# Modulation sums by block transposition, and a new first phase, in a two-block fp32 sequence kernel

## The chip, the core and the metric

One core of one Trainium2 chip runs the whole program. The metric is the device time of the core in microseconds (us), the median of several executions; beside it stands one profiled execution whose trace is read here. TensorE (PE) multiplies, VectorE (DVE) and ScalarE (ACT) work on rows of 128 partitions, GpSimd (POOL) does the few powers, SyncE (SP) issues the DMAs.

## The reference, cut to what matters

512 tokens, 1024 features, fp32, two blocks one after the other. Each block is modulated by six rows of 1024 values, made from one vector c:

```python
mod = (jax.nn.silu(c) @ w_ada[i] + b_ada[i])[:, None, :]          # w_ada: 1024 x 6144
shift_m, scale_m, gate_m, shift_f, scale_f, gate_f = jnp.split(mod, N_MOD, axis=-1)
h = rmsnorm(x, norm_mix_w[i]) * (1.0 + scale_m) + shift_m
x = x + gate_m * hybrid_mixer(h, w_in[i], conv_w[i], ...)          # proj = h @ w_in: 1024 x 8224
h = rmsnorm(x, norm_mlp_w[i]) * (1.0 + scale_f) + shift_f
x = x + gate_f * (jnp.square(jax.nn.relu(h @ w_up[i])) @ w_down[i])
...
# second block: the same form with token_mixer (mLSTM and sliding-window attention) and conv_ffn
```

The mixer of the first block is a chunked state-space scan in four groups, each with its own B, C and four x tiles, all columns of `proj`.

## The kernel before

Everything is one core's stream of matmuls. Activations stand transposed: a tile `H[j]` holds 128 features by 512 tokens. For accuracy each operand is split into a high and a low fp32r part (`hilo`, L240: ScalarE writes `whi`, VectorE `wlo`), and every product is three matmuls (`hh,whi`, `hl,whi`, `hh,wlo`) of 128x128 weights on 512 columns. An output tile of 128 columns over eight k-tiles is 24 of them. `split_w` loads 256 columns of a weight matrix into the buffers "raw" (four of them), splits them into the rings "hi" and "lo" (five each), and calls `pump`. The framework orders the instructions of each engine when the program is built, by priorities and dependences; each engine then runs its list in order.

**Modulation.** A weight matrix of 25 MB times one vector is done on VectorE: `ada_steps` (L146) takes 256 columns of w_ada in two pieces of 512 KB and adds k-tile by k-tile, scaled by silu(c), into `adacc` (128 partitions x 256), one piece at each call of `ada_next`, which `pump` and `gemm_full` make. What remains is the sum over 128 partitions. `ada_sum` (L160) takes two such `adacc`, that is four column tiles: four fp32 matmuls with a block of ones (32 columns of weights, 128 columns of data) on TensorE, a copy by ScalarE, a transposition by TensorE and an addition of the bias by VectorE into `mod`. The six rows of both blocks, without the first block's first two, are 40 units of 256 columns, so 20 such sums; `ada_until(block, row)` completes a row where it is needed.

**First phase.** The first two rows are needed before anything else. `first_ada(j)` loads their columns of k-tile j (four DMAs of 256 KB), `first_mod(j)` (L494) adds them on VectorE into two `adacc` and sums on TensorE, then copies, transposes, adds the bias and forms the gain `gm_col`. x arrives as eight DMAs of 256 KB on SyncE's queue, behind the first four of w_ada; each 128 tokens are squared and summed (ScalarE), raised to -1/2 (GpSimd), scaled to x-hat (VectorE). `h_tile` (L419) transposes x-hat's tile j on TensorE into `nps` and scales and shifts it into `H[j]`. The loop over j (L533) then adds k-tile j to six output tiles at once (B, C and the four x tiles of group 0), 18 matmuls at L544, four accumulators in PSUM buffers "pg", two in "ps" (four buffers each; `nps`, `adaps` and `colps` use "ps" too).

**After it.** Groups 0 to 3 of the scan are woven with matmuls: `xbc_items(g + 1)` makes the next group's B, C and x tiles, and `LATE` says how many of the seven remaining pool items go into each group as filling. Then follow the branch and output matrices, the MLP, and the second block in the same manner. At w_out (`gemm_full`, `script1`) the tiles of 128 tokens are normalised and transposed one by one for the MLP's first matmuls.

Of the kernel before, what the change touches and what calls it, by code (L numbers as in the profile page):

```python
# [14 lines left out]
P = 128  # L15
# [11 lines left out]
def hybrid_kernel(  # L27
# [70 lines left out]

    K = const("consts", [P, C_NEG])
    stA = stage([rows(a) for a in (c, c_2, norm_mix_w, b_ada)])  # L100
# [13 lines left out]
    xa = x.rearrange("o (t p) (q n) -> p (o t) q n", p=P, n=512)  # L114
    first_raw = [first_ada(0)]
    X = []
    for t in range(NCH):
        row = []
        for q in range(2):
            u = U("x")  # L120
            dma(out=u, in_=xa[:, t, q])
            row.append(u)
        X.append(row)
    dma(out=K[:, C_TRI:C_LAST], in_=consts[:, C_TRI:C_LAST])
# [6 lines left out]
    mhalf = const("mhalf", [P, 16])  # L131
    G.memset(mhalf, -0.5)
# [12 lines left out]

    def ada_steps(ci, col):  # L146

        acc = small("adacc", [P, 2 * P], bufs=ADB)
        for k0 in (0, 4):
            raw = RAW([P, 4, 2 * P])  # L150
            dma(out=raw, in_=ada_w[ci][0, k0 * P:(k0 + 4) * P, col * P:(col + 2) * P].rearrange("(k p) n -> p k n", p=P))
            for k in range(4):
                s_ = csil[:, 8 * ci + k0 + k:8 * ci + k0 + k + 1]
                if k0 + k == 0:
                    V.tensor_scalar(out=acc, in0=raw[:, k], scalar1=s_, scalar2=None, op0=ALU.mult)
                else:
                    V.scalar_tensor_tensor(out=acc, in0=raw[:, k], scalar=s_, in1=acc, op0=ALU.mult, op1=ALU.add)  # L157
            yield acc

    def ada_sum(ci, col, accs):  # L160

        ps = PS("adaps")
        for j in range(4):
            PE.matmul(ps[j * 32:(j + 1) * 32, 0:P], lhsT=ones[:, 0:32], rhs=accs[j // 2][:, j % 2 * P:(j % 2 + 1) * P],  # L164
                      start=True, stop=True)
        row = small("colraw", [P, P])
        act(out=row, in_=ps[:, 0:P], func=AF.Copy)
        yield
        ps = PS("adaps")
        PE.transpose(ps[:, 0:P], row, ident)  # L170
        V.tensor_tensor(out=mod[ci][:, col:col + 4], in0=ps[:, 0:P:32], in1=bcol[ci][:, col:col + 4], op=ALU.add)
        yield

    ada_todo = [(0, 8 * sec + i) for sec in (2, 4, 3, 5) for i in range(0, 8, 2)] + [(1, i) for i in range(0, 48, 2)]
    ada_now, ada_open, ada_half = [], [], []
# [8 lines left out]
    def ada_close(n):  # L184
        while ada_half:
            next(ada_half.pop(0))
        while len(ada_open) > max(n, 1):
            (ci, col), a0 = ada_open.pop(0)
            ada_half.append(ada_sum(ci, col, (a0, ada_open.pop(0)[1])))
            next(ada_half[-1])  # L190
        while ada_half and n == 0:
            next(ada_half.pop(0))

    def ada_next(hold=False):
        if ada_now:
            key, gen = ada_now.pop()
            ada_open.append((key, next(gen)))
            return
        if not hold:
            ada_close(3)  # L200
        if ada_todo and len(ada_open) < ADB - 1:
            ci, col = ada_todo.pop(0)
            ada_now.append(((ci, col), ada_steps(ci, col)))
            next(ada_now[0][1])

    def ada_until(ci, sec):
        todo = [(ci, 8 * sec + i) for i in range(0, 8, 2)]
        while any(t in todo for t in ada_todo + [t for t, _ in ada_now]):
            ada_next()
        ada_close(0)  # L210
# [271 lines left out]
    first = [wi[:, 4096:5120].rearrange("k (s g n) -> k s g n", s=2, n=P)[:, :, 0], wi[:, 2048:2560]]  # L482

    def first_w(j):
        raw = RAW([P, 768])
        o = 0
        for w in first:
            n = w.shape[-1] * (2 if len(w.shape) == 3 else 1)
            dst = raw[:, o:o + n]
            dma(out=dst.rearrange("p (s n) -> p s n", s=2) if len(w.shape) == 3 else dst, in_=w[j * P:(j + 1) * P])  # L490
            o += n
        return raw

    def first_mod(j):  # L494
        src = [first_raw[j][k // 4][:, k % 4] for k in range(8)]
        acc = [small("adacc", [P, 2 * P], bufs=ADB) for _ in range(2)]
        for k in range(8):
            c_, t = csil[:, k:k + 1], acc[k % 2]
            if k < 2:
                V.tensor_scalar(out=t, in0=src[k], scalar1=c_, scalar2=None, op0=ALU.mult)  # L500
            else:
                V.scalar_tensor_tensor(out=t, in0=src[k], scalar=c_, in1=t, op0=ALU.mult, op1=ALU.add)
        ps = PS("adaps")
        for k in range(2):
            for i in range(2):
                PE.matmul(ps[i * 64:(i + 1) * 64, 0:P], lhsT=ones[:, 0:64], rhs=acc[k][:, i * P:(i + 1) * P],
                          start=k == 0, stop=k == 1)
# [13 lines left out]
    for t in range(NCH):  # L521
        rs.append(rsqrt(row_ss(X, t), D, 1e-5, "n"))
        if t:
            xh[t - 1] = x_hat(X, t - 1, rs[t - 1], False)
# [8 lines left out]
    for j in range(8):  # L533
        if j < 7:
            raws.append(first_w(j + 1))
# [1179 lines left out]
```

## Time and profile before

| | us |
|---|---|
| median of 3 runs (1624.26 to 1624.70) | 1624.59 |
| the profiled execution's own time | 1624.09 |
| its span, first to last instruction | 1622.3 |
| TensorE matmuls busy, x7810 | 1589.5 |
| VectorE busy, x1995 | 1086.5 |
| ScalarE busy, x1275 | 715.4 |
| GpSimd busy, x47 | 28.3 |

Busy times of engines overlap. Matmuls are pipelined: each row's duration is longer than its distance to the next, so the distance between starts is the price of one in the stream. PEld are the loads of weights, beside the matmuls. The granted clock is full (0.999 in the mean).

### The profile page before, as it was taken

How to read it: one execution, taken by the hardware profiler on the slowest of the kernel's cores; microseconds unless marked ns; L12 is line 12 of the kernel's file. 1: busy time of each engine (PE TensorE's matmuls, PEld its weight loads, DVE VectorE, ACT ScalarE, POOL GpSimd, SP SyncE). 2: the span in 40 equal slices, each digit the busy share in tenths (PEclk: the TensorE clock that was granted, in tenths of full speed). 3: DMA queues.
4: the chain of work that ended last, by engine and by line, in shares of the span. 5: the costliest groups of instructions: out<-in, count | busy, mean ns of one | idle time of the engine just before them, and what ended most of it. 6: DMA issues, size and time to landing. Idle time of an engine off the chain costs nothing.

```text
span 1622.3 us, 20792 instructions
## 1 busy us (share of the span) xinstructions
PE 1589.5 (98%) x7810; PEld 1274.0 (79%) x7810; DVE 1086.5 (67%) x1995; ACT 715.4 (44%) x1275; POOL 28.3 (2%) x47
## 2 busy tenths in 40 slices
PE   5999999999999999999999999999999999999998
PEld 3778777777877878877877788887788888888886
DVE  6686897888766675876257773578876756145644
ACT  4543656555454332633214332655555643144421
POOL 0000000000000000000000000000011000000000
PEclk9999999999999999999999999999999999999999
DMA  9731544444444435466236571122331323332321
GB/s 280 197 100 59 178 142 149 130 143 138 149 130 138 142 127 177 137 196 209 96 115 197 195 252 48 53 81 76 94 102 53 103 81 102 91 104 87 96 91 53
DMA packets 206830, 206.45 MB, mean 127 GB/s; under 512 B 11469, under 2 KB 184585, under 8 KB 206729
## 3 DMA queue, kind: packets, MB, share of 16 engines
q1 hardware_dynamic: 206729, 205.12, 41.6%
q8 instruction: 61, 1.00, 0.3%
q14 instruction: 40, 0.33, 0.1%
HBM read 202.90 MB, written 2.19 MB: 126 GB/s over the span
## 4 chain that ended last, share of the span: by engine, by line
PE 90%; DVE 4%; DMA 3%; ACT 2%; issue 1%; SPq 0%; POOL 0%; DVEq 0%; POOLq 0%; ACTq 0%
PE ga L274 53%; PE gb L352 21%; PE gb L312 5%; PE go L1494 2%; PE ga L544 2%; DMA wraw<-in_w_ada_dram 1%; DMA AB<-acs 1%; DVE wlo L244 1%; PE nps L424 1%; PE yps L829 1%; PE stps L838 0%; ACT arel L803 0%; PE yps L834 0%; DMA x<-in_x_dram 0%; PE adaps L164 0%
## 5 line engine op out<-in xcount | busy, mean ns | idle before, releaser
L274 PE MATMUL ga<-hh,whi 128*128 128x512 f32 (+1 forms) x1200 | 464.6, 390 | 1.0 <-ACT hh L431 0.9
L244 DVE TENSOR_TENSOR wlo<-wraw,whi 128x1024 fp32r<-128x1024 f32 (+3 forms) x249 | 297.9, 1198 | 246.8 <-ACT whi L243 246.2
L274 PE MATMUL ga<-hl,whi 128*128 128x512 f32 (+1 forms) x1200 | 457.6, 382 | 2.2 <-DVE hl L433 2.1
L274 PE MATMUL ga<-hh,wlo 128*128 128x512 f32 (+1 forms) x1200 | 456.8, 382 | 0.0
L243 ACT ACTIVATE whi<-wraw 128x1024 fp32r<-128x1024 f32 (+3 forms) x249 | 257.5, 1036 | 335.3 <-PE gb L352 151.4
L274 PEld LDWEIGHTS ga<-hh,whi 128*128 128x128 f32 x1200 | 224.1, 188 | 54.1 <-issue 6.7
L274 PEld LDWEIGHTS ga<-hl,whi 128*128 128x128 f32 x1200 | 225.3, 188 | 50.6 <-issue 3.3
L274 PEld LDWEIGHTS ga<-hh,wlo 128*128 128x128 f32 x1200 | 225.3, 188 | 46.7
L157 DVE SCALAR_TENSOR_TENSOR adacc<-wraw,csil,adacc 128x256 f32<-128x256 f32 x280 | 133.7, 482 | 36.1 <-DMA wraw<-in_w_ada_dram 31.7
L352 PE MATMUL gb<-whi,hidh 128*128 128x512 f32 x240 | 78.2, 396 | 0.0
L352 PE MATMUL gb<-wlo,hidh 128*128 128x512 f32 x240 | 77.8, 394 | 0.0
L352 PE MATMUL gb<-whi,hidl 128*128 128x512 f32 x240 | 77.5, 394 | 0.0
L450 DVE SCALAR_TENSOR_TENSOR xs<-xraw,colB,xs 128x511 f32<-128x511 f32 (+2 forms) x72 | 53.8, 748 | 8.8 <-ACT xs L448 7.9
L352 PE MATMUL gb<-whi,fh 128*128 128x512 f32 x176 | 57.3, 396 | 0.0
L352 PE MATMUL gb<-wlo,fh 128*128 128x512 f32 x176 | 57.2, 395 | 0.0
L352 PE MATMUL gb<-whi,fl 128*128 128x512 f32 x176 | 57.0, 394 | 0.0
L352 PEld LDWEIGHTS gb<-whi,hidh 128*128 128x128 f32 x240 | 45.0, 188 | 10.8 <-issue 0.4
L803 ACT ACTIVATE arel<-AB,acs 128x128 f32<-128x128 f32 x128 | 40.7, 389 | 29.0 <-DMA AB<-acs 20.6
L352 PEld LDWEIGHTS gb<-whi,hidl 128*128 128x128 f32 x240 | 45.1, 188 | 10.7
L352 PEld LDWEIGHTS gb<-wlo,hidh 128*128 128x128 f32 x240 | 45.1, 188 | 10.4
L274 PE MATMUL ga<-yh,whi 128*128 128x512 f32 x128 | 51.1, 399 | 0.0
L274 PE MATMUL ga<-yh,wlo 128*128 128x512 f32 x128 | 50.6, 395 | 0.0
(421 smaller groups left out, 2374.2 us busy)
## 6 DMA issues: line engine op xcount, KB each, us to landing
wraw<-in_w_ada_dram SPq DMA_DIRECT2D x80, 512.0 KB
wraw<-in_w_in_dram SPq DMA_DIRECT2D x72, 512.0 KB
wraw<-in_w_down_dram SPq DMA_DIRECT2D x54, 512.0 KB
wraw<-in_w_up_dram SPq DMA_DIRECT2D x88, 256.0 KB
wraw<-in_w_up_dram SPq DMA_DIRECT2D x32, 512.0 KB
araw<-in_w_ada_dram SPq DMA_DIRECT2D x32, 256.0 KB
AB<-acs SPq DMA_DIRECT2D x32, 256.0 KB
wraw<-in_w_branch_ssd_dram SPq DMA_DIRECT2D x16, 512.0 KB
```

What stands on the lines that cost most here:

```text
L157: V.scalar_tensor_tensor(out=acc, in0=raw[:, k], scalar=s_, in1=acc, op0=ALU.mult, op1=ALU.add)
L243: act(out=hi, in_=raw, func=AF.Copy)
L244: V.tensor_tensor(out=lo, in0=raw, in1=f(hi), op=ALU.subtract)
L274: PE.matmul(ps[:, n0:n1], lhsT=a[:, m * P:(m + 1) * P], rhs=b[:, n0:n1], start=i == 0, stop=i == 3 * n - 1)
L312: PE.matmul(pss[t][:, 0:ncols], lhsT=a[:, t * P:(t + 1) * P], rhs=b, start=k == 0 and j == 0, stop=k == n - 1 and j == 2)
L352: PE.matmul(pss[t][q], lhsT=a, rhs=w[b][q], start=i == 0 and j == 0, stop=i == n - 1 and j == 2)
L424: PE.transpose(ps[:, i * P:(i + 1) * P], xh[t][j // 4][:, (j % 4) * P:(j % 4 + 1) * P], ident)
L450: V.scalar_tensor_tensor(out=o[:, d:], in0=ps[:, 0:S - d], scalar=cols[taps - 1 - d], in1=o[:, d:], op0=ALU.mult, op1=ALU.add)
L544: PE.matmul(fps[i], lhsT=a[:, i * P:(i + 1) * P], rhs=b, start=j == 0 and q == 0, stop=j == 7 and q == 2)
L803: act(out=t[:, i * P:(i + 1) * P], in_=AB[q][:, i * P:(i + 1) * P], func=AF.Relu, scale=-1.0, bias=acs[:, hh:hh + 1])
L829: PE.matmul(ps[r * 64:(r + 1) * 64, j * P:(j + 1) * P], lhsT=xdt[:, hh * 64:(hh + 1) * 64], rhs=M[hh // 4][:, (hh % 4) * P:(hh % 4 + 1) * ...
L1494: PE.matmul(opss[t][q], lhsT=x_, rhs=w[q][b_], start=half == 0 and k == 0 and j == 0, stop=half == 1 and k == 3 and j == 2)
```

## The change

The sum over partitions behind the start: a unit is now 512 columns (four pieces); VectorE transposes the 128x512 `adacc` in blocks of 32x32 and adds within each block (`adR`, 16 values a partition), so that each of four groups of 32 partitions holds a partial sum. `ada_until` adds the four with one fp32 matmul of 32 columns for a whole row of 1024 (weights `quarters`), and three small VectorE steps pick each partition's own column and add the bias.

The first phase: x of tokens 0 to 255 comes by ScalarE's queue ahead of everything, the rest on SyncE's behind the first w_ada; ScalarE's table is loaded early by a small Tanh. Statistics are made for two groups of 128 tokens at a time, half of the squares on VectorE. The modulation of k-tiles 0 and 1 is done by TensorE straight from w_ada (`first_pe`: 16 matmuls with 128x128 of w_ada as weights on one column of silu(c)); that of the later ones by ScalarE (one step) and VectorE (seven) into one `adacc`, two k-tiles ahead, with two matmuls on one column for the sum (`first_sum`) that need no transposition. The matmuls of k-tile 0 run first for tokens 0 to 255, then for 256 to 511. There are seven output tiles instead of six (B of group 1 is the seventh), three of them in "ps"; `xbc_items(1)` makes one tile less, and `LATE` gives group 0 four pool items instead of three, group 1 three instead of four.

```diff
+    load_x((0, 1), SC.dma_start)
...
     def ada_steps(ci, col):
+        acc = U("adacc")
+        for h in range(2):
+            a = acc[:, h * 2 * P:(h + 1) * 2 * P]
+            for k0 in (0, 4):
+                raw = RAW([P, 4, 2 * P])
...
+                if h and k0:
+                    tr = U("adtr")
+                    V.transpose(out=tr, in_=acc)
+                    V.tensor_reduce(out=adR[ci][:, col * 4:col * 4 + 16], in_=tr.rearrange("p (b f) -> p b f", f=32),
+                                    axis=AX.X, op=ALU.add)
+                yield
...
     def ada_until(ci, sec):
...
-        ada_close(0)
+        ps = PS("adaps")
+        PE.matmul(ps[:, 0:32], lhsT=quarters, rhs=adR[ci][:, sec * 32:sec * 32 + 32], start=True, stop=True)
...
+    NF = 7
...
+    def first_acc(j):
+
         src = [first_raw[j][k // 4][:, k % 4] for k in range(8)]
+        acc = small("adacc", [P, 2 * P], bufs=ADB)
+        act(out=acc, in_=src[0], func=AF.Copy, scale=csil[:, 0:1])
+        for k in range(1, 8):
+            V.scalar_tensor_tensor(out=acc, in0=src[k], scalar=csil[:, k:k + 1], in1=acc, op0=ALU.mult, op1=ALU.add)
+            if k == 4:
+                yield acc
+        yield acc
+
+    def first_sum(j, acc):
+
+        ps = PS("adaps")
+        for i in range(2):
+            PE.matmul(ps[:, i:i + 1], lhsT=acc[:, i * P:(i + 1) * P], rhs=ones[:, 0:1], start=True, stop=True)
+        first_mod(j, ps)
+
+    def first_pe(j):
+
+        ps = PS("adaps")
         for k in range(8):
...
+                PE.matmul(ps[:, i:i + 1], lhsT=first_raw[j][k // 4][:, k % 4, i * P:(i + 1) * P], rhs=csil[:, k:k + 1],
+                          start=k == 0 and i == 0, stop=k == 7 and i == 1)
+        first_mod(j, ps)
...
+    fps = [PG("ga") for _ in range(4)] + [PS("ga") for _ in range(NF - 4)]
...
     first_raw.append(first_ada(1))
...
+    rs[0] = first_stats((0, 1))
+    first_pe(0)
+    first_hat((0, 1), 0, (1,))
+    first_h(0, (0, 1), False)
+    ws = hilo(raws[0], [P, NF * P])
+    rs[1] = first_stats((2, 3))
+    first_hat((2, 3), 0, (3,))
+    first_mm(0, ws, range(NF), 0, 256)
+    first_h(0, (2, 3), False)
+    raws.append(first_w(1))
     first_raw.append(first_ada(2))
+    first_mm(0, ws, range(NF), 256, S)
+    first_pe(1)
     for j in range(8):
+        if j < 6:
+            raws.append(first_w(j + 2))
+            if j < 5:
+                first_raw.append(first_ada(j + 3))
+            acc = first_acc(j + 2)
+        if j:
+            first_mm(j, ws, (0, 1))
...
         if j < 7:
+            nw = hilo(raws[j + 1], [P, NF * P])
+            if j < 6:
+                next(acc)
             first_h(j + 1)
+            if j < 6:
+                a0 = next(acc)
+        if j:
+            first_mm(j, ws, range(2, NF))
+        if j < 6:
+            first_sum(j + 2, a0)
+        ws = nw
...
+ADB = 2
 SETTLE = (7, 15)
-ADB = 5
 POOLN = 1
-LATE = (3, 4, 0, 4)
+LATE = (4, 3, 0, 4)
```

TensorE's list at the start of the program, before (`adaps` is the modulation's sum, `nps` x-hat transposed, `ga` an output tile):

```order
L94 MATMUL colps<-consts,colraw 128x72
L506 MATMUL adaps<-adacc,ones 64x128 x4
L511 MATMUL adaps<-consts,colraw 128x128
L424 MATMUL nps<-consts,nx 128x128 x4
L544 MATMUL ga<-hh,whi 128x512 x4
L544 MATMUL ga<-hl,whi 128x512
```

All 512 tokens went through in one piece, four transpositions and then full-width matmuls. After, from the same place:

```order
L94 MATMUL colps<-consts,colraw 128x72
L510 MATMUL adaps<-csil,araw 128x1 x16
L416 MATMUL nps<-consts,nx 128x128 x2
L548 MATMUL ga<-hh,whi 128x256 x5
L548 MATMUL ga<-hl,whi 128x256
```

Two transpositions and 21 matmuls for 256 tokens come first. The second half of the tokens follows in TensorE's list after the change, with the second k-tile's modulation within it:

```order
L548 MATMUL ga<-hh,wlo 128x256
L416 MATMUL nps<-consts,nx 128x128 x2
L548 MATMUL ga<-hh,whi 128x256 x7
L510 MATMUL adaps<-csil,araw 128x1 x15
L548 MATMUL ga<-hl,whi 128x256
L548 MATMUL ga<-hh,wlo 128x256
```

Its other matmuls of half width, fourteen in all, stand behind those fifteen. The end of k-tile 0 and the second k-tile's beginning in the same list:

```order
L548 MATMUL ga<-hh,wlo 128x256
L510 MATMUL adaps<-csil,araw 128x1
L416 MATMUL nps<-consts,nx 128x128 x4
L548 MATMUL ga<-hh,whi 128x512 x5
L548 MATMUL ga<-hl,whi 128x512
L548 MATMUL ga<-hh,wlo 128x512
L502 MATMUL adaps<-ones,adacc 128x1 x2
```

The sixteenth matmul of that modulation stands after all half-width ones, and the second k-tile's transpositions after it.

TensorE's list where the first block's MLP turns from w_up (`ga`) to w_down (`gb`), before:

```order
L274 MATMUL ga<-hh,wlo 128x512
L170 MATMUL adaps<-consts,colraw 128x128
L164 MATMUL adaps<-adacc,ones 32x128 x4
L352 MATMUL gb<-whi,hidh 128x512
L352 MATMUL gb<-wlo,hidh 128x512
L352 MATMUL gb<-whi,hidl 128x512
```

and after, at the same place:

```order
L266 MATMUL ga<-hh,wlo 128x512
L196 MATMUL adaps<-adR_114,quarters 128x32
L344 MATMUL gb<-whi,hidh 128x512
L344 MATMUL gb<-wlo,hidh 128x512
L344 MATMUL gb<-whi,hidl 128x512
```

Of the sums one matmul is left. Over the whole program the 20 sums (14 alone, 3 times two together) become ten matmuls at six places.

VectorE's list at w_out, before (`tmp` and `x` belong to the last 128 tokens, `ntmp` and `hl` to h for the MLP, `adacc` to the modulation):

```order
L432 TENSOR_SCALAR ntmp<-nps,gc_f,mod_115 128x256 [waits Activation_49]
L157 SCALAR_TENSOR_TENSOR adacc<-wraw,csil,adacc 128x256 [waits DMAHW3_49]
L433 TENSOR_TENSOR hl<-ntmp,hh 128x256 [waits DVE_49]
L1022 TENSOR_TENSOR tmp<-gb,gm 128x512 x2
L1023 TENSOR_TENSOR x<-x,tmp 128x512 [waits DVE_49] x2
```

and after:

```order
L424 TENSOR_SCALAR ntmp<-nps,gc_f,mod_112 128x256 [waits Activation_49]
L425 TENSOR_TENSOR hl<-ntmp,hh 128x256 [waits DVE_49]
L1077 TENSOR_TENSOR tmp<-gb,gm 128x512 x2
L1078 TENSOR_TENSOR x<-x,tmp 128x512 [waits DVE_49] x2
L236 TENSOR_TENSOR wlo<-wraw,whi 128x1024 [waits DMAHW7_49,Activation_49]
```

The modulation step that waits for its DMA stood between `ntmp` and `hl`; now none stands there.

## Rows read from the trace of the kernel before

**Rows 1.** The page, busy us, share of the span and instructions of each engine.
```profile
PE 1589.5 (98%) x7810; PEld 1274.0 (79%) x7810; DVE 1086.5 (67%) x1995; ACT 715.4 (44%) x1275; POOL 28.3 (2%) x47
```

**Rows 2.** Busy time by stretch; columns: stretch, length, each engine, PEclk, DMA share, GB/s.
```profile
0.00:20.00 20.00, 3.38 (x13) 1.66 (x13) 8.46 (x32) 7.74 (x21) 2.70 (x11) 1.00 0.86 255
20.00:40.00 20.00, 17.89 (x88) 12.62 (x89) 17.67 (x47) 8.69 (x14) 0.00 (x0) 1.00 1.19 304
...
220.00:240.00 20.00, 19.30 (x114) 15.74 (x114) 19.81 (x32) 13.20 (x24) 0.00 (x0) 1.00 0.41 121
...
660.00:680.00 20.00, 17.25 (x134) 15.95 (x135) 16.74 (x39) 12.42 (x27) 0.99 (x1) 1.00 0.39 123
```

**Rows 3.** TensorE's timeline, start and end of the first phase: start, duration, instruction, idle before.
```profile
22.11 2.07 PE L544 MATMUL ga<-hh,whi 128*128 128x512 f32 x4 [1.53 <-ACT hh L429]
23.99 0.63 PE L544 MATMUL ga<-hl,whi 128*128 128x512 f32 x1
24.41 0.63 PE L544 MATMUL ga<-hh,wlo 128*128 128x512 f32 x1
...
67.66 0.27 PE L94 MATMUL colps<-consts,colraw 120*128 120x120 f32 x1
```

**Rows 4.** The chain that ended last, first phase: start, length, engine, tile and line.
```profile
47.11 0.59 PE adaps L506 x8
...
48.82 0.11 PE adaps L511
48.93 0.44 PE nps L424 x4
```

**Rows 5.** The chain at the turn to the MLP and within it.
```profile
607.26 0.57 PE adaps L164 x16
...
608.73 0.22 PE adaps L170 x2
...
695.51 0.35 PE adaps L164 x8
695.86 11.35 PE ga L274 x48
707.22 0.11 PE adaps L170
707.33 11.16 PE ga L274 x48
```

**Rows 6.** The chain at a group's normalisation: four fp32 matmuls on one column.
```profile
285.38 0.79 PE ssps L865 x8
```

**Rows 7.** Busy time by stretch, as rows 2; the last column is GB/s.
```profile
7.50:10.00 2.50, 0.00 (x0) 0.00 (x0) 1.77 (x5) 0.00 (x0) 0.00 (x0) 1.00 0.94 281
25.00:30.00 5.00, 4.53 (x27) 2.98 (x25) 3.75 (x11) 2.43 (x4) 0.00 (x0) 1.00 1.19 304
```

**Rows 8.** Timelines of VectorE and of GpSimd in the first 20 us.
```profile
8.95 1.67 DVE L502 SCALAR_TENSOR_TENSOR adacc<-araw,csil,adacc 128x256 f32<-128x256 f32 x4 [0.73 <-DMA araw<-in_w_ada_dram]
12.57 0.16 DVE L513 SCALAR_TENSOR_TENSOR gm_col<-mod,colA 128x1 f32<-128x1 f32 x1
...
18.98 0.55 POOL L396 TENSOR_TENSOR nr<-nv,mhalf 128x1 f32<-128x1 f32 x1 [1.25 <-DVE nv L394]
```

**Rows 9.** Groups by shape: busy us, mean ns of one, idle before.
```profile
L1318 DVE TENSOR_REDUCE amx<-sm 128x4 f32<-128x512 f32 x8 | 5.5, 682 | 0.1
L450 DVE SCALAR_TENSOR_TENSOR xs<-xraw,colB,xs 128x511 f32<-128x511 f32 x24 | 18.0, 748 | 7.9 <-ACT xs L448 7.9
L396 POOL TENSOR_TENSOR gr<-gv,mhalf 128x4 f32<-128x4 f32 x8 | 9.2, 1146 | 557.1 <-DVE gv L394 549.0 <-DVE mdn L1438 8.1
L428 ACT ACTIVATE ntmp<-nps,mod,gm_col 128x512 f32<-128x512 f32 x8 | 6.2, 780 | 7.1 <-DVE gm_col L513 4.3 <-PE nps L424 2.7
```

**Rows 10.** Timelines of VectorE and of TensorE after w_out.
```profile
660.69 0.48 DVE L157 SCALAR_TENSOR_TENSOR adacc<-wraw,csil,adacc 128x256 f32<-128x256 f32 x1 [1.75 <-DMA wraw<-in_w_ada_dram]
661.57 0.39 PE L274 MATMUL ga<-hl,whi 128*128 128x256 f32 x1 [2.13 <-DVE hl L433]
```

More of the change, by code (lines that the diff above doesn't have):

```diff
@@ L97, in columns, with load_x @@
         return t
+    xa = x.rearrange("o (t p) (q n) -> p (o t) q n", p=P, n=512)
+    X = [[U("x") for _ in range(2)] for _ in range(NCH)]
+    def load_x(ts, queue):
+        for q in range(2):
+            for t in ts:
+                queue(out=X[t][q], in_=xa[:, t, q])
     K = const("consts", [P, C_NEG])
+    mhalf = const("mhalf", [P, 16])
+    G.memset(mhalf, -0.5)
+    act(out=small("atab", [P, 1]), in_=mhalf[:, 0:1], func=AF.Tanh)
+    load_x((0, 1), SC.dma_start)
     stA = stage([rows(a) for a in (c, c_2, norm_mix_w, b_ada)])
@@ L144, in hybrid_kernel @@
     ada_w, bcol = [w_ada, w_ada_2], [ba_col, None]
+    adR = [const("adR1", [P, 192]), const("adR2", [P, 192])]
     def ada_steps(ci, col):
[L148 to L172, printed above, removed]
@@ L491, in first_w @@
             o += n
         return raw
-    def first_mod(j):
+    def first_acc(j):
         src = [first_raw[j][k // 4][:, k % 4] for k in range(8)]
-        acc = [small("adacc", [P, 2 * P], bufs=ADB) for _ in range(2)]
-        for k in range(8):
[L498 to L504, printed above, removed]
-            for i in range(2):
-                PE.matmul(ps[i * 64:(i + 1) * 64, 0:P], lhsT=ones[:, 0:64], rhs=acc[k][:, i * P:(i + 1) * P],
-                          start=k == 0, stop=k == 1)
-        row = small("colraw", [P, P])
-        act(out=row, in_=ps[:, 0:P], func=AF.Copy)
-        ps = PS("adaps")
-        PE.transpose(ps[:, 0:P], row, ident)
-        V.tensor_tensor(out=mod[0][:, j:j + 9:8], in0=ps[:, 0:P:64], in1=ba_col[:, j:j + 9:8], op=ALU.add)
+        acc = small("adacc", [P, 2 * P], bufs=ADB)
[5 more added lines that the diff above has]
+        yield acc
@@ new lines, in hybrid_kernel, with first_mm @@
+    fps = [PG("ga") for _ in range(4)] + [PS("ga") for _ in range(NF - 4)]
+    def first_mm(j, w, tiles, n0=0, n1=S):
+        for i in tiles:
+            for q, (a, b) in enumerate(((w[0], H[j][0]), (w[0], H[j][1]), (w[1], H[j][0]))):
+                PE.matmul(fps[i][:, n0:n1], lhsT=a[:, i * P:(i + 1) * P], rhs=b[:, n0:n1], start=j == 0 and q == 0 and n0 == 0,
+                          stop=j == 7 and q == 2)
+    for q in range(2):
+        for t in (2, 3):
+            dma(out=X[t][q], in_=xa[:, t, q])
+        if q == 0:
+            raws = [first_w(0)]
```

135 lines of the change are left out of this document (66 added, 69 removed).

## The prediction

> **What bounds the kernel now.** I read the page's busy lines first, then busy time in 20-us stretches, then the waits and the chain where TensorE stood idle. TensorE is busy 98% of the span [rows 1]. Of the 32.8 us in which it is not (1622.3 less 1589.5), the first 40 us hold 18.7 (16.6 and 2.1) and the stretch from 660 holds 2.75 [rows 2]; most of the rest lies at the very end, and nearly everywhere else it is full. So the time is TensorE's work, plus the start, plus one gap near 660. [...]
>
> **The unit.** In a stretch of plain 512-column matmuls 48 of them take 11.16 us [rows 5], 0.2325 each; 24 of them, one output tile of eight k-tiles, are 5.6 us.
>
> **Part 1, the modulation sums behind the start.** Before, each of 20 groups of four columns costs TensorE four fp32 matmuls with ones (eight instructions) and a transposition. The chain prices them: from the beginning of one sum (695.51) to the end of the transposition and on to the next plain stretch (707.33) are 11.82 us, of which 48 matmuls are 11.16, so 0.66 a group [rows 5]. By the order fourteen groups stand alone: 9.2 us. Six stand in pairs; a pair shows 0.57 and 0.22 in the chain [rows 5], with about 0.2 for the break in the stream 1.0, so three pairs 3.0. Together 12.2 us, all in stretches where TensorE has no idle time to give. The change puts ten matmuls in their place, 128x128 fp32 weights on 32 columns. This shape is not in the trace; the nearest is the sum of squares, the same weights on one column: 0.79 us for four matmuls [rows 6], 0.2 each. Ten are 2.0, and six breaks of 0.1 make 2.6; bounds are 1 (the transposition's 0.11 each, [rows 5]) and 4. **Net -9.6 us, between -8 and -11.** VectorE takes the work over: 20 block transpositions and 20 reductions of 128x512. The reduction is 0.68 [rows 9]; a transposition is not in the trace, I take 0.68 too, bounds 0.4 and 0.75 (the scalar-times-tensor operation of 511 columns [rows 9]). So 1.3 us a unit, 26 us in all. I cost it at nothing: VectorE is busy 67% of the span [rows 1], and by the order each reduction stands several VectorE rows ahead of the matmul that reads it. Only about six units fall into 170 to 520, where VectorE is nearly full (19.81 of 20 us from 220 [rows 2]). If that cover fails there, 6 x 1.3 = 8 us at most; I keep 3 of it for the range. ScalarE only loses copies.
>
> **Part 2, the first phase.** It ends before the change at 67.66, when the next transposition starts [rows 3]. Seven tiles make the phase's own share 24 matmuls larger and take the same 24 out of group 1 later (LATE moves one pool item forward, so that group 0 keeps its filling). So the number to beat is 67.66 + 5.6 = 73.2. I build the new end from S, the start of the second k-tile's matmuls.
>
> First k-tile. The first modulation now needs 1.05 MB of w_ada, with the first token pair of x (1.05 MB, ScalarE's queue) and some of the second pair ahead of it or beside it. Before, its last pieces were there at 8.95 [rows 8]. The bytes flow at 281 GB/s early and 304 later [rows 7], whichever queue issues, and one more MB is 3.6 us; x starts about 1 us sooner, so 11.4, between 10 and 12.5. TensorE multiplies 16 blocks by one column at 0.2 [rows 6]; eight are left after the last piece, 1.6 us, or 3.2 at half speed: 13.8. VectorE adds the bias and forms the gain (two steps of 0.16 [rows 8]), and only then comes to its two squares at 0.75 [rows 9] and two small steps, with the waits between them 0.4: 16.0. GpSimd's power, x-hat, transpositions and h took 3.1 us before, from 18.98 [rows 8] to the first matmul at 22.11 [rows 3]; half the width and one step less on ScalarE save 0.8 (the step's 0.78 [rows 9]), two columns instead of one on GpSimd add 0.2 (one column 0.55 [rows 8], four 1.15 [rows 9]): first matmul at 18.5 instead of 22.1. The second pair repeats this behind VectorE's rest of the first: 1.0, then squares, small steps and 2.5 again, 23.9. Then TensorE runs in order seven half-width matmuls (0.12), fifteen of the second modulation's matmuls (0.2), fourteen half-width ones, the sixteenth: 0.8 + 3.0 + 1.7 + 0.2 = 5.7, so 29.6. Bias and gain 0.3, transpositions 0.44 [rows 4], partly beside each other, and two ScalarE steps, 0.78 [rows 9] and a narrower one that I put at 0.65: **S = 31.6.**
>
> From there 147 matmuls are 34.2 us. Each of six k-tiles adds four transpositions, 0.44 [rows 4], and two sums on one column, 0.5 with the break [rows 6]; before, a k-tile paid 0.59 + 0.11 and two breaks [rows 4], 0.9. End: 31.6 + 34.2 + 6 x 0.94 = 71.4. **Net 71.4 - 73.2 = -1.8 us.** Other engines keep up from the third k-tile on: VectorE's share is seven steps at 0.42 [rows 8], a split of 896 columns and h's lower half of 512 (1.2 and 0.7 by the reduction's 0.68 for 512 [rows 9]) and small ones, 5.1 against TensorE's 5.8; DMA brings 1.5 MB a k-tile at 304 GB/s [rows 7], 4.9 us. One thing may add: seven accumulators leave one "ps" buffer of four, so the sum and the transpositions of h take turns, and the transpositions wait for VectorE's bias step, which stands behind modulation steps that wait for w_ada. I cost it at 0, at most 0.5 a k-tile, 3 us. With S between 27.5 and 36 the phase gives -6 to +2.6.
>
> [...]
>
> **Part 3, the gap near 660.** TensorE waited 2.13 us for h's lower half [rows 10]; VectorE stood before it at a modulation step whose w_ada piece landed late (1.75 idle, then 0.48 [rows 10]). With the new modulation order the steps stand one piece earlier: by the order no such step is left between these rows. What is late next is the chain of x-hat through GpSimd, a few tenths behind. **-1.6 us, between 0 and -2.5.**
>
> Small edits (consts later, table load early, the weights' split of one tile) sit beside busy TensorE: 0, bounds -0.5 and +1.
>
> **Sum.** -9.6 - 1.8 - 1.6 = -13.0 on the profiled run's own 1624.09 (span 1622.3 and 1.8 around it) gives 1611.1; the median of the runs, 1624.59, lies 0.5 higher: **1611.6 us**.
>
> **The rivals.** (a) *The early start pays in full*: w_ada lands at 10, the array is fast, S is 27.5, the phase gives -6: 1607.4. For it: TensorE is nearly empty for 20 us. Against: VectorE and TensorE work this start in order, each behind the other. [...] (c) *VectorE becomes the bound*: all 20 units on the path are 26 us, less the 13 gained, +13: 1637.6, slower. It decides from the tenth unit on the path. Against: only some six lie where VectorE is nearly full. (d) *The change doesn't do what it says*: TensorE, rid of the sums, waits as long for weights' splits or h, and the start is not earlier: 1621.5 to 1624.6. For it VectorE's full stretch; against, TensorE is full outside the gaps, VectorE only in places [rows 1, 2].
>
> **How the numbers follow.** Forecast 0.60 (own range 1608 to 1615), (a) 0.15, (b) 0.12, (c) 0.04, (d) 0.07, the rest 0.02. The range 1604.5 to 1618.5 takes in (a) and (b) with the bounds of parts 1 to 3 that can fall together and leaves (c) and (d) out. About 0.2% (3.2 us) is what a measurement of this kernel can tell from no change: faster 0.88, within 0.07, slower 0.05.
>
> **What would show it.** Part 1: ten matmuls of 32 columns, 0.2 to 0.3 each, none with a wait; no transposition of modulation rows; block transposition near 0.7. Part 2: first full matmul near 18.5, second k-tile near 31.6, end of the phase near 71.4. Part 3: no wait of 2 us for h's lower half near 648. I am wrong if TensorE's busy time does not fall by about 10 us, if a modulation matmul waits for VectorE, or if the phase ends after 75.

## The result, and the profile after

The changed kernel takes **1615.3 us** (median of four executions, 1612.08 to 1617.46) against 1624.64 for the kernel before on the same chip: ratio 0.9939, 95% interval 0.9921 to 0.9957, 9.3 us less. The forecast was 1611.6, with 1604.5 to 1618.5 as its range. The executions of the kernel before lie within 1.7 us of each other, those of the changed one within 5.4; the profiled one is the slowest of the four, 1617.46 (span 1615.7, mean granted clock 0.995).

First the page's engine line, which answers to [rows 1]: TensorE's matmuls are 123 fewer, and yet busy 2.0 us longer.

```profile
PE 1591.5 (99%) x7687; PEld 1289.8 (80%) x7687; DVE 1100.6 (68%) x2028; ACT 711.3 (44%) x1250; POOL 26.8 (2%) x45
```

Busy time by stretch answers to [rows 2] (columns as there; the eighth figure is the granted clock).

```profile
0.00:20.00 20.00, 8.30 (x36) 7.64 (x36) 4.81 (x19) 5.57 (x12) 1.19 (x8) 1.00 0.94 284
20.00:40.00 20.00, 17.56 (x89) 16.48 (x89) 9.21 (x23) 6.23 (x12) 0.70 (x1) 0.79 0.78 211
40.00:60.00 20.00, 20.00 (x101) 16.54 (x100) 17.39 (x41) 9.82 (x15) 0.00 (x0) 0.96 0.87 252
...
640.00:680.00 40.00, 39.36 (x270) 35.27 (x269) 31.14 (x65) 24.98 (x49) 1.64 (x3) 1.00 0.30 94
```

Before, the granted clock read 1.00 in every stretch. Now it reads 0.79 from 20 to 40 and 0.96 from 40 to 60. The chain of waits through the first phase (start, length, what) gives the steps that the prediction named:

```profile
8.43 6.57 PE adaps L510 x30
...
15.39 1.23 DVE njunk L523 x4
...
18.52 0.72 PE nps L416 x2
...
19.88 4.85 PE ga L548 x21
...
25.62 1.09 PE ga L548 x7
26.71 4.86 PE adaps L510 x30
31.57 3.20 PE ga L548 x14
...
35.94 0.79 ACT ntmp L420
...
36.75 0.64 ACT hh L421
...
37.43 2.65 PE ga L548 x7
```

The second k-tile begins at 37.43, forecast 31.6. The first phase ends at 78.59, where the transposition stands that ended it at 67.66 before [rows 3]: 5.3 us more than the 73.26 that the seventh tile would make of the old end, and 7.2 more than the forecast 71.4. This trace is of the slowest execution; in a second trace of the same kernel, at 1615.73 us, the second k-tile begins at 36.74 and the phase ends at 77.91. The same stretch by the granted clock:

```profile
8.43:15.00 6.57, 6.56 (x30) 6.47 (x30) 0.00 (x0) 0.95 (x1) 0.00 (x0) 1.00 1.09 355
19.88:24.70 4.82, 4.82 (x23) 4.82 (x23) 2.99 (x9) 1.89 (x5) 0.70 (x1) 1.00 1.18 308
25.00:28.00 3.00, 2.38 (x21) 2.38 (x21) 2.29 (x5) 1.80 (x3) 0.00 (x0) 1.00 1.18 301
28.00:34.60 6.60, 6.60 (x33) 6.60 (x33) 0.05 (x1) 0.00 (x0) 0.00 (x0) 0.50 0.33 99
...
38.00:41.60 3.60, 3.60 (x13) 2.87 (x12) 1.89 (x7) 0.62 (x1) 0.00 (x0) 0.54 1.01 287
41.60:78.60 37.00, 37.00 (x184) 30.32 (x182) 29.66 (x60) 20.88 (x31) 0.00 (x0) 1.00 0.66 184
```

From 28.0 to 34.6 and from 38.0 to 41.6 the granted clock reads 0.50 and 0.54 (called half clock below). From 8.43 to 24.7 it reads 1.00, but the spacing says otherwise: the first burst's 21 half-width matmuls take 4.85, 0.23 each, as much as the fourteen (3.20 at 31.57) for which it does read 0.50, and the 30 instructions of the first modulation take 0.22 each, where the second's, begun at a granted 1.00, take 0.16. TensorE looked busy there (4.82 of 4.82 us from 19.88), with its matmuls as far apart as at 0.50.

Behind the first phase the traces show a little more than was forecast. Two rows, each from the copy of the dt product (the end of the first phase) to the end of the program, of the kernel before and of the one after:

```profile
71.60:1622.30 1550.70, 1536.67 (x7528) 1237.28 (x7528) 1037.29 (x1870) 680.65 (x1211) 25.59 (x36) 1.00 0.40 121
```

```profile
82.50:1615.70 1533.20, 1523.17 (x7344) 1232.94 (x7344) 1054.45 (x1922) 675.29 (x1191) 24.94 (x36) 1.00 0.40 123
```

The 24 matmuls that moved forward are 5.6 us. With them the rest is 1538.8 against 1550.7: **-11.9**, forecast -9.6 and -1.6. The two parts balance: +5.3 and -11.9 are the 6.6 us between the two spans. One trace doesn't fix the -11.9. Two more rows, of the second trace of the same kernel from the same place on, and of 5 us of the first:

```profile
81.82:1613.90 1532.08, 1521.75 (x7344) 1231.85 (x7344) 1054.01 (x1922) 675.21 (x1191) 24.96 (x36) 1.00 0.40 123
```

```profile
1079.00:1084.00 5.00, 5.00 (x19) 4.04 (x20) 4.11 (x15) 2.86 (x12) 0.00 (x0) 0.66 0.00 0
```

In the second trace the rest is 1537.7 with the 5.6, so -13.0. The first trace holds a third stretch at half clock, in mid-program (0.50 from 1079.4 to 1082.8): 0.66 over 5 us is an estimated loss of up to 1.7, more than the difference. From 1074.3 to 1079.2 TensorE had transpositions and matmuls on 4 to 128 columns before it, and two on 512; in the second trace the clock reads 1.00 there (1060 to 1100). Over the kernels below that change only the start, the same figure goes from -10.1 to -14.1.

What stands in the place of the old sums (the chain, and the groups by shape): four instructions, two of the new matmuls, take 0.36, and VectorE's block transposition 0.706.

```profile
608.43 0.36 PE adaps L196 x4
...
926.46 0.37 PE adaps L196 x4
```

```profile
L165 DVE STREAM_TRANSPOSE adtr<-adacc 128x512 f32<-128x512 f32 x20 | 14.1, 706 | 0.1
...
L166 DVE TENSOR_REDUCE adR<-adtr 128x16 f32<-128x512 f32 x20 | 13.6, 678 | 0.1
```

### The profile page after: what moved, and what is told of

Read it like the earlier page. It is cut to its first block, busy times and chain, and to the rows that moved or that the text cites. A ratio compares the mean times of both kernels' runs of the same rounds, so it can differ in the third digit from the quotient of the medians.

```text
span 1615.7 us, 20548 instructions
## 1 busy us (share of the span) xinstructions
PE 1591.5 (99%) x7687; PEld 1289.8 (80%) x7687; DVE 1100.6 (68%) x2028; ACT 711.3 (44%) x1250; POOL 26.8 (2%) x45
## 4 chain that ended last, share of the span: by engine, by line
PE 94%; DVE 3%; ACT 1%; DMA 1%; issue 0%; POOL 0%; SPq 0%; DVEq 0%; POOLq 0%; ACTq 0%
PE ga L266 56%; PE gb L344 21%; PE gb L304 4%; PE ga L548 3%; PE go L1549 2%; PE yps L884 1%; PE stps L893 1%; PE nps L416 1%; PE adaps L510 1%; PE yps L889 1%; PE xtps L845 0%; DVE wlo L236 0%; DMA araw<-in_w_ada_dram 0%; DVE qk L442 0%; PE sps L1363 0%
## 5 line engine op out<-in xcount | busy, mean ns | idle before, releaser
L266 PE MATMUL ga<-hh,whi 128*128 128x512 f32 (+1 forms) x1192 | 459.2, 388 | 0.7 <-ACT hh L423 0.6
L162 DVE SCALAR_TENSOR_TENSOR adacc<-wraw,csil,adacc 128x256 f32<-128x256 f32 x280 | 130.2, 481 | 17.1 <-DMA wraw<-in_w_ada_dram 14.7
L344 PEld LDWEIGHTS gb<-whi,hidl 128*128 128x128 f32 x240 | 45.1, 188 | 10.7
L266 PE MATMUL ga<-yl,whi 128*128 128x512 f32 x128 | 50.4, 393 | 0.0
```

The source lines that it names most:

```text
L162: V.scalar_tensor_tensor(out=a, in0=raw[:, k], scalar=s_, in1=a, op0=ALU.mult, op1=ALU.add)
L266: PE.matmul(ps[:, n0:n1], lhsT=a[:, m * P:(m + 1) * P], rhs=b[:, n0:n1], start=i == 0, stop=i == 3 * n - 1)
L344: PE.matmul(pss[t][q], lhsT=a, rhs=w[b][q], start=i == 0 and j == 0, stop=i == n - 1 and j == 2)
```

## The experiments

Each ratio is against the kernel before, run in turn with the kernel on the same chip; the kernel after was run again beside three of them (second modulation off, both off, VectorE's part doubled).

### The two halves apart

**The sums alone.** The kernel before with `ada_steps` and `ada_until` of the kernel after, `LATE`, six tiles and first phase as before.

```diff
-    def ada_sum(ci, col, accs):
...
+                    V.transpose(out=tr, in_=acc)
+                    V.tensor_reduce(out=adR[ci][:, col * 4:col * 4 + 16], ...)
...
-ADB = 5
+ADB = 3
```

> The kernel before with the new modulation sums alone (block transposition, ten matmuls of 32 columns); first phase, six tiles and LATE as before, the ring of adacc cut from five to three for space. Theory (sums and the gap near 660 pay as forecast, the new first phase is what fell short): -9.6 - 1.6 = -11.2 on 1624.6, so 1613.4; the profiled runs of before and after leave 6.6 + 5.5 = 12.1 outside the first phase, which would be 1612.5. The granted clock stays as before, 0.999, and the runs lie within 1 us of each other. Rival (the sums gave little, the first phase gave the 9.3): 1622 or more.

Measured: 1615.16 (1614.52 to 1616.72), ratio 0.9938, interval 0.9926 to 0.9950: 10.1 less. In its trace the first phase ends 1.95 later than before (69.61 for 67.66), since the first matmuls of 512 columns stand 0.42 apart up to 26.5 instead of 24.4 [rows 3]; from there on:

```profile
73.50:1613.00 1539.50, 1529.25 (x7368) 1236.14 (x7368) 1056.40 (x1920) 676.88 (x1191) 24.96 (x36) 1.00 0.40 122
```

1539.5 against 1550.7 is -11.2, the forecast of the two parts; that it fits to a tenth is luck, since two traces of the kernel after lie 1.1 apart in this stretch. TensorE's busy time there falls by 7.4, its idle time from 14.0 to 10.25. The whole kernel misses its 1613.4 by 1.8, about what the phase lost. So parts 1 and 3 stand by themselves, without the new phase, and give as much as the whole change.

**The phase alone.** The kernel after with the old sums, one buffer fewer in the pool of 512-column tiles.

```diff
-    adR = [const("adR1", [P, 192]), const("adR2", [P, 192])]
+    def ada_sum(ci, col, accs):
...
-UB = 64
+UB = 63
-ADB = 2
+ADB = 5
```

> The kernel after with the old modulation sums (ones-matmuls, copy, transposition), so the new first phase alone; one buffer fewer among the 512-column tiles, for space. Theory: the phase costs TensorE time, 5.5 us in the profiled run of after (78.75 against 67.66 + 5.6 before) and two to three less where the clock is granted more: 1626.5 to 1630, with runs several us apart and a granted clock under 0.999. Rival (the phase gives its 1.8 and it was the sums that fell short): 1622.8.

Measured: 1636.45 (1631.15 to 1639.27), ratio 1.0064, interval 1.0049 to 1.0080: 11.1 slower, more than either theory gave. Its profiled execution (1631.15) explains half: the phase ends at 76.78, 3.5 above 73.26, and the rest is 3.6 longer than before, with holes such as these (before: TensorE is busy for all 20.00 from 240, and for 17.25 from 660 [rows 2]).

```profile
240.00:260.00 20.00, 18.57 (x112) 14.94 (x111) 19.01 (x34) 12.38 (x28) 0.00 (x0) 1.00 0.62 184
660.00:680.00 20.00, 16.70 (x130) 15.01 (x129) 16.41 (x36) 11.65 (x25) 1.05 (x1) 1.00 0.52 159
```

The median's other 5 us were not caught in a trace; they stay open, as does the share of the buffer taken away. That the new phase ends later than the old one would is shown in this trace too; what the rest of the 11.1 is made of is not.

### The clock or the order

**TensorE kept at work.** The kernel after with products of zeros laid into the holes of the start and the second modulation's instructions between the half-width matmuls, to see whether the stretches at a granted clock of 0.50 go when TensorE is kept at work.

```diff
+    warm(8)
     colA = columns("colA", stA)
+    warm(12)
...
-    first_pe(0)
+    first_pe(0, lambda k: warm(1))
+    warm(12)
...
-    first_mm(0, ws, range(NF), 256, S)
-    first_pe(1)
+    some(5)
+    first_pe(1, lambda k: some(2))
```

> The kernel after with TensorE kept at work in the start: multiplications of zeros by zeros on 512 columns (8 before the first transposition, 12 ahead of the first modulation, one after each of its k-tiles, 12 behind it, 2 and 2 before the half-width bursts, 5 before the second k-tile), and the second modulation's matmuls laid between the half-width ones; what they add is zero. [...] Rival (dependences, not the clock: the first modulation waits for bytes and VectorE's squares stand behind it): second k-tile not before 35.5, time within 1.5 of the kernel after, 1614 to 1617.

**VectorE's squares first.** One edge in VectorE's list.

```diff
-    first_pe(0)
-    first_hat((0, 1), 0, (1,))
+    hat = first_hat((0, 1), 0, (1,))
+    with tc.issue_after(hat):
+        first_pe(0)
```

> The kernel after with VectorE's two squares of the first token pair and its x-hat queued ahead of the bias step that waits for TensorE's first modulation; nothing else. Theory (order): the wait of 3.5 us for x-hat at 18.5 goes, transpositions start at 15.0, first half-width matmul at 16.4 instead of 19.9, second k-tile at 34, time 3.4 less than the kernel after: about 1612. Rival (the clock takes it): the early part is earlier, but as the same half-width burst and the same one-column matmuls follow, the clock is withdrawn as before and for as long or longer; second k-tile at 36 or later, time 1614 to 1616.

Measured: fillers 1616.06 (1613.29 to 1618.78), ratio 0.9941, interval 0.9929 to 0.9953; squares first 1614.34 (1612.26 to 1616.29), ratio 0.9935, interval 0.9922 to 0.9948. Neither is apart from the kernel after (0.9939). The chain of squares-first shows that its order did what was asked:

```profile
16.34 4.68 PE ga L549 x21
...
21.90 1.09 PE ga L549 x7
22.99 5.12 PE adaps L510 x30
28.11 3.05 PE ga L549 x14
...
33.72 2.89 PE ga L549 x7
```

All steps are 3.5 to 3.7 us earlier than in the first trace of the kernel after and 3.0 earlier than in the second, the phase ends at 74.92, and yet the granted clock falls again, at 24.0, 1.0 us behind the start of the second modulation (0.50 from 24.0 to 30.5). The five executions have mean clocks from 0.994 to 0.999. The fillers' profiled execution (the fastest of its five) shows the granted clock where they worked and where not:

```profile
10.00:15.00 5.00, 5.00 (x44) 4.54 (x42) 0.82 (x4) 0.77 (x1) 0.70 (x1) 1.00 1.07 358
25.00:29.90 4.90, 4.90 (x46) 4.90 (x45) 2.54 (x5) 0.70 (x2) 0.00 (x0) 1.00 1.14 305
30.00:33.80 3.80, 3.80 (x16) 2.50 (x14) 2.94 (x8) 1.60 (x3) 0.00 (x0) 0.56 0.61 178
```

From 10.2 to 14.6 the first modulation's 32 instructions run with eight 512-column products among them in 4.4, 0.09 each between the products, where the 32 alone took 7, 0.22 each. The second k-tile begins at 34.4, earlier than the rival's 35.5; the rival has a part in it, since x-hat of the second pair now stands on ScalarE behind a modulation step that waits for w_ada (22.25 in the chain). But behind 25 to 29.9, all busy and half of it one-column matmuls, the granted clock fell, to 0.56 in the mean of 30 to 33.8; the other four executions had mean clocks of 0.993 to 0.995. So the first modulation's 7 us were not its own price, but the cure fails: with work in the holes the granted clock still fell, and the median, 1616.06, is no lower than the kernel after's 1615.3.

### What loses the clock

**Second modulation off TensorE.** Squares first, and the second k-tile's modulation made as the later ones are.

```diff
-    first_pe(1)
+    first_sum(1, [acc for acc in first_acc(1)][-1])
```

> The kernel with VectorE's squares ahead (e4_squares), and the second k-tile's modulation made as the later ones are, by ScalarE and VectorE with two one-column matmuls, in place of TensorE's 32 instructions on one column. Theory (these instructions lose the clock and hold the second k-tile back): in e4_squares the second k-tile begins at 33.7 behind 5.1 us of them at half clock; without them the modulation is there at about 26, second k-tile at 28 to 29, phase end near 70 instead of 75.1, so 5 less: 1609 where e4_squares took 1614.3. The clock may still be withdrawn once, since TensorE now waits some 4 us before the second k-tile. Rival (any hole costs the same clock): second k-tile earlier, but its first 8 us at half clock, 1612 to 1614.

**Both modulations off TensorE.** The kernel after, reordered.

```diff
-    first_pe(0)
+    first_sum(0, [acc for acc in first_acc(0)][-1])
...
-    rs[1] = first_stats((2, 3))
+    rs[1] = first_stats((2, 3), True)
+    acc1 = [acc for acc in first_acc(1)][-1]
...
-    first_pe(1)
+    first_sum(1, acc1)
```

> The kernel after with both first modulations made by ScalarE and VectorE (no 128x128 blocks of w_ada on TensorE at all), the second pair's squares all on ScalarE, and the second modulation ahead of the second token pair in the order. Theory: the first modulation needs no clock: last piece of w_ada near 11, VectorE's steps end at 13, bias 13.5, first half-width matmul 14.6, second modulation 21.3, second k-tile at 25 to 26, phase end 66 to 67.5: 8 less than e4_squares, 1604 to 1607. Rival (VectorE, now with sixteen modulation steps before the second k-tile, becomes the bound of the start): second k-tile at 29 or later, 1609 or more.

**The kernel after again.** 

> The kernel after again, beside the others of this call, for a second profile of its start and for how far its runs lie apart. Theory (the grant of the clock in the start falls differently from run to run): 1612 to 1618 as before, a mean granted clock of 0.995 to 0.998, a higher clock with a lower time, about 1.6 us for each 0.001; second k-tile's start between 34 and 38. Rival (the spread has nothing to do with the clock): no such order between clock and time.

Measured in this group: the kernel after 1618.02 (1614.44 to 1618.55), ratio 0.9952, interval 0.9940 to 0.9964; second modulation off 1607.37 (1606.76 to 1608.54), ratio 0.9894, interval 0.9879 to 0.9908; both off 1610.49 (1609.21 to 1611.06), ratio 0.9910, interval 0.9897 to 0.9923. The chain with the second modulation off:

```profile
8.65 6.56 PE adaps L510 x30
...
16.62 4.86 PE ga L549 x21
...
23.80 0.58 PE adaps L502 x4
24.38 1.75 PE ga L549 x14
...
28.10 1.77 PE ga L549 x6
```

The second k-tile begins at 28.10, as expected, the phase ends at 68.22, and behind the first burst, which is as slow here too (21 in 4.86, 0.23 each), the next fourteen half-width matmuls take 1.75, 0.13 each, and the granted clock reads 1.00 to the end of the phase, although TensorE still stands idle for 1.5 us before 28.1. All four executions lie within 1.8 us, with clocks of 0.998 and 0.999. This one edit is worth about 7 us against squares-first; with the squares' order the two edits are 10.7 against the kernel after beside them.

With both off, the phase ends no earlier (68.47): VectorE's list puts its squares behind the seven modulation steps, and x-hat of the first pair comes at 16.16, 5 us later than in squares-first. The second k-tile begins at 28.5, not at 25 to 26, and the time is the rival's. Its other 2 us are behind the phase, unexplained.

The kernel after's own five executions order by clock but for one: 0.996 at 1614.44 and 1615.73, 0.995 at 1618.02, 0.994 at 1618.55, but also 0.999 at 1618.55. So the order that was expected is there with one exception, and the two slowest lie above the expected range. What made the exception slow isn't known.

**Columns.** The kernel after with the same 64 instructions on 128 equal columns; further edits only hold TensorE's list in the same order.

```diff
-                PE.matmul(ps[:, i:i + 1], lhsT=..., rhs=csil[:, k:k + 1],
+                PE.matmul(ps[:, i * P:(i + 1) * P], lhsT=..., rhs=csil[:, k:k + 1].to_broadcast([P, P]),
```

> The kernel after with the two modulations on TensorE made on 128 equal columns instead of one: the same 64 instructions with the same weights at the same places of TensorE's list, only more columns each (VectorE has one of its squares ahead of the bias, 0.7 us earlier). Theory (what loses the clock is that TensorE had only single columns to multiply for 5 us): the granted clock does not fall behind them, the second modulation's 30 instructions take 3 to 3.5 us instead of 5.1, second k-tile at 32 to 34 instead of 36.7 to 37.4, at full clock, phase end 73 to 75, time 4 to 5 under the kernel after, runs within 2 us of each other, mean clock 0.998 or more. Rival 1 (the idle holes lose it, or the many weight loads): granted clock 0.50 in the same places, time as the kernel after, 1615 to 1618. Rival 2 (columns cost): the instructions grow by more than the clock gives back, later than after.

Measured: 1609.88 (1609.17 to 1611.32), ratio 0.9905, interval 0.9890 to 0.9920, all four with a clock of 0.997; phase end 74.28, the second k-tile a little later than expected. The two modulations in the chain, and the granted clock around the second:

```profile
9.63 6.46 PE adaps L510 x30
...
26.08 1.10 PE ga L577 x7
27.18 3.35 PE adaps L510 x30
30.53 1.65 PE ga L577 x14
```

```profile
19.00:25.60 6.60, 5.77 (x25) 5.06 (x24) 3.73 (x10) 2.64 (x7) 0.70 (x1) 0.50 1.14 311
25.60:32.40 6.80, 6.32 (x53) 6.13 (x53) 5.18 (x10) 2.17 (x4) 0.00 (x0) 0.98 0.78 218
34.85:74.28 39.43, 39.43 (x195) 32.69 (x196) 31.16 (x62) 22.88 (x34) 0.00 (x0) 1.00 0.82 229
```

In the second modulation the same instructions with 128 times the columns take 3.35 instead of 4.86, and behind them the clock stays (1.00 from 34.85 to 74.28). The first gains nothing: 6.46, still 0.22 each, for 0.11 in the second. The clock falls once, at 19.0, after TensorE stood idle from 16.1 to 18.8: rival 1 has its part too, and with it the mean clock is 0.997, not the expected 0.998. But the 6.6 us at half clock (0.50 from 19.0 to 25.6) lie in a burst behind which little waits (the second pair's x-hat is there at 24.1, the burst ends at 25.0), and the second k-tile (34.85) runs at a granted 1.00 from its first matmul, although TensorE stood idle for 1.5 us before it, as long as in the kernel after.

**Both cures.** Second modulation off, the first on 128 columns. 

> The kernel of e5_dve1 with the remaining modulation on TensorE, the first, on 128 equal columns instead of one. [...] Rival (the clock comes no earlier, or the second modulation's bytes and VectorE's steps set the second k-tile): 28 as before, 1607 to 1608.

Measured: 1607.08 (1606.27 to 1607.20), ratio 0.9885, interval 0.9869 to 0.9902; beside it the kernel with the second modulation off once more:

> The kernel of e5_dve1 once more, beside the others of this call. Theory: 1606.5 to 1608.5, mean clock 0.998 to 0.999, second k-tile at 28. Rival (its first measurement was a lucky grant of the clock): 1610 or more in some runs, with a mean clock under 0.998.

1607.69 (1606.83 to 1610.09), ratio 0.9893, interval 0.9878 to 0.9908. The wide first modulation ends earlier (13.15 for 15.21) and the first burst is done in 2.96 us of TensorE's busy time (4.86 without the wide columns), but then TensorE waits 2.3 us for VectorE's squares of the second pair, and behind the hole the clock reads 0.50:

```profile
11.00:13.00 2.00, 2.00 (x19) 1.91 (x17) 0.49 (x1) 0.00 (x0) 0.29 (x1) 1.00 1.07 377
13.00:21.40 8.40, 3.45 (x25) 2.78 (x23) 6.09 (x17) 4.51 (x9) 0.93 (x1) 1.00 1.18 314
21.50:28.00 6.50, 5.84 (x27) 5.51 (x27) 5.05 (x13) 1.80 (x3) 0.00 (x0) 0.50 1.18 309
```

Second k-tile at 30.3, later than 28.1. What was gained early was lost later: the time is the rival's, 1607 to 1608, the second k-tile later than its 28. The phase even ends later (70.32 against 68.22 and 67.73 in the two traces of the kernel beside it); the rest of the trace is about as much shorter, unexplained, and no difference is left between the two. Both beat the kernel after and the kernel before.

### Two smaller terms

**VectorE's part doubled.** The kernel after with `V.transpose(out=tr, in_=acc)` written twice. 

> The kernel after with each of the twenty block transpositions of the modulation sums made twice (the second writes the same values again): 14.1 us more of VectorE's time, one cause alone. Theory (VectorE's part of the sums is hidden by TensorE's work): within 2 us of the kernel after. Rival (VectorE is the bound where these stand): +7 where half of them lie on the path, +14 where all do.

Measured: 1620.08 (1616.52 to 1625.73), ratio 0.9967, interval 0.9958 to 0.9976, against 0.9952 of the kernel after beside it: 2.1 of the 14.1 us, and the intervals overlap. Most is hidden. Its waits show where some comes through (in the kernel after's traces at most 0.5 for the first, 0.2 for the second):

```profile
PE rowps L209 <- DVE mod L203: 1.9, 1, 1.9
...
PE nps L417 <- DVE ntmp L425: 1.1, 1, 1.1
```

The trace is of the slowest of the twelve executions, with two more stretches of a lower granted clock in mid-program (0.91 in the means of 740 to 760 and of 1080 to 1100); how much of the 2.1 is VectorE's and how much the clock's is not shown.

**One queue.** The kernel with the second modulation off, x of the first pair on SyncE's queue.

```diff
-    load_x((0, 1), SC.dma_start)
...
     first_raw = [first_ada(0)]
+    load_x((0, 1), dma)
```

> The kernel of e5_dve1 with the first token pair of x on SyncE's queue behind the first w_ada, as before the change, instead of ScalarE's queue ahead of it. Theory (bytes flow at one rate whichever queue issues, and the first modulation at half clock is what the start waits for): w_ada is complete 2 us earlier, the first modulation ends at 13.5 to 14.5, x of the first pair lands at 12.5, both chains meet at the same place, 1606.5 to 1608.5. Rival (the second queue is worth its issue time, four issues of 0.43 ahead of everything else): second k-tile 2 later, 1609 to 1610.

Measured: 1609.28 (1608.45 to 1611.75), ratio 0.9903, interval 0.9888 to 0.9917, against 0.9893 beside it; second k-tile at 29.83 for 28.10 in the first trace with the second modulation off. The rival: in its trace the first k-tile's weights are there 2 us later (ScalarE begins to split them at 15.6, for 13.5 with both cures), behind x's issues on SyncE's queue; those of w_ada ahead of them take 0.43 to 0.51 each in its chain. The bytes do not flow at one rate either: 291, 289 and 330 GB/s in the three microseconds from 8 to 11, and 302, 347 and 361 with the two queues (second modulation off). The second queue is worth about 1.6 us here, though the intervals overlap.

## Why the prediction was right, and where it was not

- **Sign and range**: right. Of its cases the forecast (1608 to 1615) is missed by a hair, and its account of part 2 is not what happened; case (b), a TensorE that is slow until S, was my estimate, given 0.12, and is nearest (S 37.4 for its 37, the phase +5.3 for its +3.6, with a granted clock of 0.54 for another 3.6 us from 38.0). The trace does not show it slow all the way: the first burst took 0.23 a half-width matmul, the seven from 25.62 on 0.16 each, and from 28.0 the granted clock read 0.50. The range held because it had been drawn to take in (b).
- **Part 1, -9.6**: the mechanism is right, and the size as far as the traces agree. Behind the phase TensorE's busy time fell by 7.4 with the sums alone, by 7.9 in the first trace of the kernel after (1536.67 against 1523.17 and 5.6), which holds the third stretch at half clock, and by 9.3 in the second (1521.75). The new matmuls cost what was put: 0.18 each in the chain, 1.8 for ten. Why the sums alone gave only 7.4, under the bound of 8, stays open. VectorE's unit is 0.706 and 0.678, put at 0.68 each, and its cover mostly holds: doubled, 2 of 14 us show. The price of 0.66 a group, taken from one group [rows 5], is borne out by the next, 718.49 to 730.31 in the chain before, which is 11.82 us for 48 matmuls and a sum again:

```profile
718.49 0.35 PE adaps L164 x8
...
730.20 0.11 PE adaps L170
```

- **Part 3, -1.6**: right in kind, too small. The 2.13 us [rows 10] are gone, and no wait of TensorE from 640 to 680 is longer than 0.3; its idle time there falls from 3.32 to 0.64. With the smaller holes elsewhere idle time behind the phase falls by 4.0 (14.0 to 10.0) and in the second trace by 3.7. Together the two parts gave 11.2, 11.9 and 13.0 in three traces, for 11.2.
- **Part 2, -1.8**: wrong, +5.3 in the profiled execution and +4.7 in the second trace. The steps up to the second half came 1.2 to 1.7 late (first modulation 15.0 for 13.8, first matmul 19.9 for 18.5, second half 25.6 for 23.9); the first modulation was not late for its bytes, since from 8.43 its 30 instructions ran without a wait, 0.22 each. No run shows the mean of full and half speed that the 13.8 holds for the last eight blocks; it was my estimate. Nor was the rate of the bytes one whichever queue issues: from 7.5 to 10.0 it was 281 GB/s before [rows 7] and 333 after, with two queues. The step that failed most is the next, from there to the second k-tile: 7.7 put, 11.8 measured. From the second k-tile to the end it is 41.2 for 39.8. The three make up the 7.2. I priced a 128x128 block on one column at 0.2 (two instructions, [rows 6]) and a half-width matmul at 0.12; both are right in the second modulation and behind it in the kernel with 128 columns, where the granted clock reads 1.00 (0.22 and 0.12), and about double in the kernel after, 0.44 in the first modulation and 0.23 in the half-width matmuls at a granted 0.50. The many small instructions, which I had taken to speak against a slow TensorE, were themselves what came before the fall: the granted clock fell at 28.0, 1.3 us into the second modulation, and with 128 columns in the same places it did not. The next fall, at 38.0, came behind a hole of 1.5 us; with 128 columns, and with the second modulation off, a hole as long before the second k-tile was followed by none.
- **Busy and slow**: from 8.43 to 15.0 TensorE was busy 6.56 of 6.57 us, and the next burst still took 4.85 us, 0.23 a matmul, where I had put 0.12. Nor did every hole cost the clock: it read 0.50 behind the holes that end at 18.8 (128 columns) and 21.4 (both cures), and 1.00 behind the one of 1.5 us before 28.1 (second modulation off). When it falls is not settled by these runs.
- **Squares behind the bias step**: seen (16.0), and costed. Undoing it gave 3.0 to 3.7 us in the traces and too little in the median to tell. Whether it shows where the clock is kept was not run by itself.
- **PS buffer, 0**: right. From the second k-tile to the end the phase takes 40.1 with the second modulation off, at a granted clock of 1.00, 39.8 put.
- **The signs of being wrong**: two of the three that the prediction named came. The phase ended after 75 (78.59 and 77.91), and TensorE's busy time did not fall by about 10 (it rose by 2.0); the second sign was a bad one, since busy time counts the stretches at half clock too (6.60 of 6.60 us from 28.0).

## What to carry to other kernels

Work that is moved to TensorE early is not priced by what it costs in mid-stream: look first at the spacing of its neighbours and at what runs before it. Here the first full-width matmuls of the kernel before stood 0.42 apart, for 0.23 in mid-stream, and the granted clock fell to 0.50 within the second modulation on TensorE, and read 1.00 there with that one made off TensorE. A busy TensorE is not a fast one (here 4.82 of 4.82 us, at 0.23 a half-width matmul for 0.12); read the granted clock and the distance between starts beside the busy share, and check the executions' spread (5.4 us here, 1.7 before). And read a saving from more than one execution: two traces of the same kernel lay 1.1 us apart behind the start, and one of them had a granted clock of 0.50 for 3.4 us in mid-program.

## What the runs showed that I had not expected

- 64 fp32 instructions with 128x128 weights on one column: 0.22 each in the first modulation, and the granted clock at 0.50 soon after the second began. The same on 128 columns: 0.22 each in the first as well, but 0.11 each in the second, the clock at 1.00 through it, 1609.88 us instead of 1615 to 1618.
- The granted clock reads 1.00 from the program's first microsecond to 28.0, while half-width matmuls stand 0.21 apart, for 0.12 in the kernel with 128 columns: only the spacing shows the first slow stretch.
- The 3.0 to 3.7 us that the squares' order gained in the traced starts can't be told from nothing in the medians (1614.3 against 1615.3 and 1618.0, intervals that overlap).
- The half clock is not only a matter of the start: the kernel after ran 3.4 us at it (0.50) from 1079.4 on in one trace and not in the other (1.00 from 1060 to 1100).
- Not settled: one execution of the kernel after and one of squares-first took 1618.55 and 1615.77 us at a mean granted clock of 0.999; and the phase with the old sums is 5 us slower in its median than in its traced execution.
